# First layer of the compressed keys and values in four 32-column groups, summed by a transposing product

## The chip, the cores and the metric

The kernel runs on one core of one Trainium2 chip. The metric is the device time of one execution in microseconds (us); lower is better. TensorE (PE) multiplies, VectorE (DVE) and ScalarE (ACT) work elementwise, GpSimd (POOL) does small things, and SyncE (SP) issues most of the transfers (DMA).

## The reference, cut to what matters

A decoder trunk of two layers for one sequence of 256 positions and width 1024: attention and a recurrent branch side by side, then a feed-forward part (dense in layer 0, experts in layer 1). One branch of the attention works on compressed keys and values: every window of 32 positions with stride 16 (15 of them per head) is flattened to 2048 numbers and goes through a small two-layer network.

```python
def compress_blocks(kv, pos, w1, w2):
    b_, g_, t_, _ = kv.shape
    ...
    flat = (blocks + pos).reshape(b_, g_, n_cmp, L_CMP * HEAD_DIM)
    return jax.nn.gelu(flat @ w1) @ w2
...
    kc = compress_blocks(grp(k_cmp), cmp_pos[0], cmp_w1[0], cmp_w2[0])
    vc = compress_blocks(grp(v_cmp), cmp_pos[1], cmp_w1[1], cmp_w2[1])
```

`w1` is 2048 x 128, `w2` 128 x 64; keys and values have their own. There are two heads, so keys and values together have 2 x 2 x 15 rows (padded to 2 x 32).

## The kernel before, in words

**Weights.** All weights come from memory as pieces in a fixed list. `emit_load` (line 231) issues a piece's transfer on SP's queue into one of 7 slots of `raw`; `emit_split` and `split_piece` turn a slot into halves of `hl` (5 slots): ACT copies the rounded upper part (line 280), DVE subtracts it and leaves the lower part (line 281). `use` hands a piece to its products and has those of the next piece made. A product with split operands is three PE products (`mm3`, all through `MM`, line 295): upper x upper, upper x lower, lower x upper. The two `w1` pieces of a layer (1 MB each) are not split; they stay in their `raw` slots until their products are done.

**The start.** The 256 positions are two blocks of 128. For each, `Norm.part` squares and sums two halves of a row on ACT and adds up on DVE (`rv`, line 465), `rstd` takes the root on POOL, `scale` (line 481) writes `xn` on DVE in two halves, and `tr` transposes it on PE (line 491) and splits it into `hT` (ACT 495, DVE 496). The first projection, `mixers`' values (`vps`), multiplies `hT` with the two `v` pieces of `w_in`.

**A layer's mixer** (`mixers`, from line 570). In the order of the code: values; recurrent input; `kcvc`; first half of the queries; gates; `flat` (line 731, the windows plus the position term, laid out as 16 chunks of 128 x 32 for keys and for values); `k`; `rg_out(0)`; **the first layer of the compressed keys and values**; `rg_out(1)`; its transpose (line 747) and the second layer; scores and softmax; output projection (`wor`, `woa`). `rg_out` projects a half of the gate branch (48 PE records), applies a Gelu on ACT (`gy`, line 669), multiplies on DVE (670), and makes `sq`, `rech` (ACT) and `recl` (DVE, 677).

**The first layer before.** For keys, then values, 16 products of a chunk (128 x 32, the stationary operand) with 128 rows of `w1` add up in PSUM partitions 0-31 and 32-63. ACT takes the Gelu of the 64 x 128 result into `hid` (744). After `rg_out(1)`, PE transposes `hid` (747) and DVE copies it to `hidt` (749) and spreads the values' part to `vst` (751); both feed the second layer (`w2s`).

**What follows it.** `scores(c)`, four times: PE makes `s`, DVE adds `bias` and takes the minimum in one instruction (792), ACT takes exp (796), DVE scales (803). The softmax over the compressed keys, `pc`, is a chain of DVE steps (854 to 868) with one exp; PE transposes `pc` (882) before the first `attend`.

**What sets the order.** A list scheduler under the code orders each engine's queue; the code's order is its starting point, and `tc.issue_after` holds the instructions in its block behind a named one. So an edit can move instructions that the diff does not touch.

Of the kernel before, what the change touches and what calls it, by code (L numbers as in the profile page):

```python
# [9 lines left out]
F32 = mybir.dt.float32  # L10
# [3 lines left out]
AF = mybir.ActivationFunctionType  # L14
ALU = mybir.AluOpType
# [3 lines left out]
P = 128  # L19
# [35 lines left out]
def f32(ap):  # L55
    return ap.bitcast(F32)
# [3 lines left out]
def decoder_trunk(ctx, tc, x, p, attn_norm, w_in, cmp_pos, cmp_w1, cmp_w2, conv_w, conv_b, lru_wa, lru_ba,  # L60
                  lru_wx, lru_bx, lru_lambda, out_norm_attn, out_norm_rec, w_out, ffn_norm, dense_w_gate,
                  dense_w_up, dense_w_down, router_w, moe_w_gate, moe_w_up, moe_w_down, ple_norm, ple_w_gate,
                  ple_w_proj, final_norm, out, stop=None):
    nc = tc.nc

    const = ctx.enter_context(tc.tile_pool(name="const", bufs=1))
# [6 lines left out]
    def uid(s):  # L73
        cnt[0] += 1
        return f"{s}_{cnt[0]}"

    def pst(s="ps"):
        return psum.tile([P, 512], F32, name=uid(s), tag="ps")
# [116 lines left out]
    keys = {pc[0]: n for n, pc in enumerate(pieces)}  # L195
# [40 lines left out]
    def emit_split(upto):  # L236

        while nsplit[0] <= min(upto, len(pieces) - 1):
            key, srcs, kc, n, split = pieces[nsplit[0]]
            emit_load(nsplit[0])  # L240
            nsplit[0] += 1
            if key[:2] != (DEPTH - 1, "pg"):
                split_piece(key, kc, n, split)
# [43 lines left out]
    def use(*key, ahead=None):  # L287
        emit_split(keys[key] + (depth[0] if ahead is None else ahead))
        split_piece(*[pieces[keys[key]][m] for m in (0, 2, 3, 4)])
        return ready.pop(key)  # L290
# [3 lines left out]
    def MM(*args, **kw):  # L294
        r = nc.tensor.matmul(*args, **kw)  # L295
        if pinned[0]:
            pinned[0] = False
            tc.keep_in_program_order(r)
        return r
# [41 lines left out]
    nc.gpsimd.iota(jp, pattern=[[1, P]], base=0, channel_multiplier=-1, allow_small_or_imprecise_dtypes=True)  # L341
    ident = const.tile([P, P], F32)
    nc.vector.tensor_scalar(ident, jp, 0.0, None, op0=ALU.is_equal)
    tri = const.tile([P, P], F32)
    nc.vector.tensor_scalar(tri, jp, 0.0, None, op0=ALU.is_gt)
    mhalf = const.tile([P, 1], F32)
# [180 lines left out]
    def proj_t(w):  # L527

        ps = pst()
        for ch in range(2):  # L530
            for k in range(KC):
                mm3(ps[:, ch * T:(ch + 1) * T], [v[:, k] for v in w[ch]], (hT[0][:, k, :], hT[1][:, k, :]),
                    k == 0, k == KC - 1)
        return ps
# [40 lines left out]
    def mixers(i, wk, norm, nxt):  # L575
# [7 lines left out]
        flat = [wk.tile([P, 16, 2, 16], F32, name=uid("flat"), tag="flat", bufs=2) for _ in range(2)]  # L583
        qt = wk.tile([P, 4, T], F32, name=uid("qt"), tag="qt", bufs=1)
        kt = wk.tile([P, 2, T], F32, name=uid("kt"), tag="kt", bufs=1)
        bd = wk.tile([P, 2, 4, P], F32, name=uid("bd"), tag="bd", bufs=1)
        hid = wk.tile([64, P], F32, name=uid("hid"), tag="hid", bufs=1)
        wk.tile([P, 1], F32, name=uid("rg"), tag="rg", bufs=NRG)

        vt = wk.tile([P, NB, T], F32, name=uid("vt"), tag="vt", bufs=1)  # L590
# [68 lines left out]
        def rg_scan(hf, a, th, ig, u):  # L659
            nc.scalar.activation(th[sl], th[sl], AF.Sqrt, scale=-0.25)  # L660
            nc.vector.tensor_tensor(ig[sl], ig[sl], th[sl], op=ALU.mult)
            for c in range(2):
                nc.vector.tensor_tensor_scan(u[:, c, :T], a[:, c, :T], ig[:, c, :T], 0.0, op0=ALU.mult, op1=ALU.add)
            return u

        def rg_out(hf, u):
            ps = proj_t(use(i, "yg", hf))
            gy = rgt("gy")
            nc.scalar.activation(gy[:, :, :T], ps.rearrange("p (c t) -> p c t", c=2), AF.Gelu_apprx_tanh)
            nc.vector.tensor_tensor(u[sl], u[sl], gy[sl], op=ALU.mult)  # L670
            sq = rgt("sq", (2, T))
            nc.scalar.activation(sq, u[sl], AF.Square)
            rsq.append(sq)
            for c in range(2):
                cc = 2 * hf + c
                nc.scalar.activation(rec_h[:, cc], u[:, c, :T], AF.Copy, scale=prm(64, cc))
                nc.vector.scalar_tensor_tensor(rec_l[:, cc], u[:, c, :T], prm(64, cc), f32(rec_h[:, cc]),
                                               op0=ALU.mult, op1=ALU.subtract)
# [24 lines left out]
        ps = proj_t(use(i, "kcvc"))  # L703
# [18 lines left out]
        for kv in range(2):  # L722
            ps = pst()
# [10 lines left out]
        ps = proj_t(use(i, "k"))  # L734
        nc.scalar.activation(kt, ps.rearrange("p (v t) -> p v t", v=2), AF.Copy)
        u = [rg_scan(hf, *dec[hf]) for hf in range(2)]
        rg_out(0, u[0])
        hps = pst()
        for kv in range(2):
            w1 = use(i, "w1", kv)  # L740
            for c in range(16):
                MM(hps[kv * 32:kv * 32 + 32, :P], lhsT=flat[kv][:, c].rearrange("p g c -> p (g c)"), rhs=w1[:, c],
                   start=(c == 0), stop=(c == 15))
        nc.scalar.activation(hid, hps[:64, :P], AF.Gelu_apprx_tanh)
        rg_out(1, u[1])
        ps = pst()
        nc.tensor.transpose(ps[:, :64], hid, ident[:64, :64])
        hidt = wk.tile([P, 2, 2, 16], F32, name=uid("hidt"), tag="hidt", bufs=1)
        nc.vector.tensor_copy(hidt, ps[:, :64].rearrange("p (v g c) -> p v g c", v=2, g=2))
        vst = wk.tile([P, 2, 4, 16], F32, name=uid("vst"), tag="vst", bufs=1)  # L750
        nc.vector.tensor_copy(vst, hidt[:, 1, :, None, :].to_broadcast([P, 2, 4, 16]))
        ps = pst()
# [90 lines left out]
        p0 = scores(0)  # L843
# [3 lines left out]
        for c in range(4):  # L847
            for b in range(NB):
                o = (c * 2 + b) * 32
                MM(cps[:, o:o + 32], lhsT=qt[:, c, b * P:(b + 1) * P], rhs=kcb.rearrange("p g k -> p (g k)"),  # L850
                   start=True, stop=True)
# [28 lines left out]
        ps = pst()  # L880
# [20 lines left out]
        norm = Norm(nxt)  # L901
# [24 lines left out]
        for b in range(NB):  # L926
            for hf in range(2):
                if b == 0:
                    ps = ps0[hf]
                    wo_mm(ps, att, b, w[hf], (3,))  # L930
                else:
                    ps = pst()
# [15 lines left out]
            if router and b:  # L948
# [5 lines left out]
                r = norm.rstd(b)  # L954
                for hf in range(2):
                    v = norm.x[b][:, hf * 512:hf * 512 + 512]
# [614 lines left out]
    def dump():  # L1571
        for b in range(NB):
            nc.sync.dma_start(out[0, b * P:(b + 1) * P, :], xt[:, b])

    norm = Norm(None, gain0)
    for b in range(NB):
        for hf in range(2):
            norm.half(b, hf)
        norm.scale(b)
        if b == 0:  # L1580
            norm.tr(b)
    for i in range(DEPTH):
        with tc.tile_pool(name=f"att{i}", bufs=1, reuse_waits="tile") as wk:
            norm = mixers(i, wk, norm, ffn_norm[i])
        if stop == f"mix{i}":
            return dump()
        with tc.tile_pool(name=f"ffn{i}", bufs=1, reuse_waits="tile") as wk:
            if i == 0:
                ppj, prev = dense(i, wk, norm)
            else:  # L1590
                more = [(hpool, "hT0", 1), (hpool, "hT1", 1)] + [(ring, "raw", NRAW)] * (NRAW - NEARLY)
                more += [(bpool, "bias", 1)] + [(wk, "raw2", NRAW2)] * NRAW2 + [(ring, "hl", NSPL)] * NSPL
                more += [(ring, "raw", NRAW)] * NEARLY
                slots[:] = itertools.cycle(more), wk
                moe(i, wk, norm)
            if i == 0 and stop != "ffn0":
                norm = Norm(attn_norm[i + 1])
                ple(i, wk, ppj, prev, norm)
        if stop == f"ffn{i}":
            return dump()  # L1600
        if stop == f"ple{i}":
            return dump()
# [30 lines left out]
```

## Time and profile before

| | us |
|---|---|
| median of 3 runs | 1388.51 (1386.14 to 1388.85) |
| the profiled execution | 1390.27 |
| its span, first to last instruction | 1388.6 |
| around the span | 1.67 |
| mean granted TensorE clock | 0.984 of full speed |

The profile is of one execution, 1.76 us above the median of the runs. PE is busy for 93% of the span, DVE 45%, ACT 37%, POOL 3%. In the page's 40 slices of 34.7 us, the DMA engines stand at 9 tenths or more in the first two slices, at 1 to 6 tenths in the third to the fourteenth, and at 9 or more again from the fifteenth to the last but one. A busy PE is not PE at its peak: the ends of matmuls are modelled. A product in full 32-bit floats leaves two records per instruction in the trace, so the 32 products of a first layer are 64 records.

### The profile page before, as it was taken

To read this page: it belongs to the slowest core of one execution; us is meant where nothing else is said; L and a number is where in the kernel's file an instruction comes from. 1 tells how busy PE (TensorE), PEld (TensorE's weight loads), DVE (VectorE), ACT (ScalarE), POOL (GpSimd) and SP (SyncE) were. 2 spreads that over 40 slices of the span, in tenths; PEclk is the share of its full clock that TensorE was granted. 3 is DMA by queue.
4 is the path that set the end of the run, shared out by engine and by line. 5 is a ranking of instruction groups with operands and counts; after the bars stand their busy time and mean duration, and the time that the engine had idled before them with its cause. 6 is when DMAs were issued, how large, how long until landed. Compare 5 with 4: busy or idle time off the path is not lost. (4 is left out here: it accounts for less than half of the span.)

```text
span 1388.6 us, 18284 instructions
## 1 busy us (share of the span) xinstructions
PE 1296.0 (93%) x7056; PEld 825.1 (59%) x7056; DVE 618.4 (45%) x1036; ACT 514.5 (37%) x808; POOL 35.8 (3%) x72
## 2 busy tenths in 40 slices
PE   7999999999999989999999999999879788788996
PEld 6977899998897743568753468854323222233432
DVE  7866655546777530278841178842010011013203
ACT  5665544445566520357730157740000010002103
POOL 2000000000100000000000000000000000000000
PEclk9999999999999999999999999999989999999998
DMA  9941555554646399999999999999999999999992
GB/s 281 265 132 62 205 184 190 192 192 125 203 141 165 124 394 404 396 393 394 402 408 410 396 394 395 395 410 409 402 408 409 402 409 381 394 403 403 393 390 99
DMA packets 180615, 435.83 MB, mean 314 GB/s; under 512 B 8841, under 2 KB 59177, under 8 KB 180522
## 3 DMA queue, kind: packets, MB, share of 16 engines
q1 hardware_dynamic: 178984, 430.92, 83.4%
q0 software_dynamic: 992, 3.15, 0.7%
q8 instruction: 58, 0.95, 0.3%
q10 hardware_dynamic: 546, 0.53, 0.1%
q14 instruction: 35, 0.29, 0.1%
HBM read 433.51 MB, written 1.05 MB: 313 GB/s over the span
## 5 line engine op out<-in xcount | busy, mean ns | idle before, releaser
L281 DVE TENSOR_TENSOR hl<-raw,hl 128x1024 fp32r<-128x1024 f32 (+1 forms) x294 | 343.9, 1206 | 147.6 <-ACT hl L280 141.8
L295 PE MATMUL gu<-raw,x 128*64 128x512 f32 (+1 forms) x1536 | 315.4, 554 | 36.9 <-DMA raw<-in_moe_w_up_dram 15.0
L280 ACT ACTIVATE hl<-raw 128x1024 fp32r<-128x1024 f32 (+1 forms) x294 | 294.2, 1043 | 113.5 <-PE ps L295 67.2
L295 PEld LDWEIGHTS gu<-raw,x 128*64 128x64 f32 x1536 | 107.2, 139 | 225.6 <-issue 158.5
L295 PE MATMUL ps<-hT,hl 128*128 128x256 f32 x1824 | 221.5, 281 | 1.2 <-ACT hT L495 0.8
L295 PEld LDWEIGHTS ps<-hT,hl 128*128 128x128 f32 x1824 | 217.9, 188 | 4.0 <-ACT hT L495 1.0
L1286 DVE TENSOR_TENSOR sl<-sl,gu 128x512 f32<-128x512 f32 (+1 forms) x24 | 14.9, 621 | 414.9 <-PE gu L295 381.9
L295 PE MATMUL y<-raw,at 128*64 128x512 f32 x672 | 157.3, 599 | 8.0 <-DMA raw<-in_moe_w_down_dram 7.9
L295 PE MATMUL gu<-hl,xh 128*128 128x512 f32 x448 | 144.4, 398 | 1.9 <-ACT hl L280 1.7
L295 PEld LDWEIGHTS y<-raw,at 128*64 128x64 f32 x672 | 45.2, 136 | 100.3 <-issue 78.5
L295 PEld LDWEIGHTS gu<-hl,xh 128*128 128x128 f32 x448 | 83.7, 188 | 34.1 <-DVE hl L281 9.5
L1285 ACT ACTIVATE sl<-gu 128x512 f32<-128x512 f32 (+1 forms) x24 | 13.1, 544 | 240.0 <-PE gu L295 240.0
L295 PE MATMUL gu<-hl,xl 128*128 128x512 f32 x224 | 88.0, 393 | 0.0
L295 PE MATMUL y<-hl,ah 128*128 128x512 f32 x224 | 73.2, 399 | 0.0
L295 PE MATMUL ps<-hl,hT 128*128 128x512 f32 (+1 forms) x288 | 64.9, 377 | 0.5 <-ACT hT L524 0.5
L1295 ACT ACTIVATE at<-ps 128x512 f32<-128x512 f32 (+1 forms) x24 | 13.1, 544 | 132.5 <-PE ps L1293 132.5
L295 PEld LDWEIGHTS ps<-hl,hT 128*128 128x128 f32 x288 | 49.7, 197 | 19.8 <-issue 10.0
L295 PE MATMUL acc<-hl,ah 128*128 128x512 f32 x176 | 55.5, 397 | 0.0
L295 PEld LDWEIGHTS y<-hl,ah 128*128 128x128 f32 x224 | 41.6, 188 | 10.8 <-issue 1.6
L295 PEld LDWEIGHTS gu<-hl,xl 128*128 128x128 f32 x224 | 42.1, 188 | 8.1
L295 PE MATMUL y<-hl,al 128*128 128x512 f32 x112 | 43.9, 392 | 0.0
L295 PEld LDWEIGHTS acc<-hl,ah 128*128 128x128 f32 x176 | 32.2, 188 | 6.9
(312 smaller groups left out, 1091.4 us busy)
## 6 DMA issues: line engine op xcount, KB each, us to landing
raw<-in_moe_w_gate_dram SPq DMA_DIRECT2D x112, 1024.0 KB
raw<-in_moe_w_up_dram SPq DMA_DIRECT2D x112, 1024.0 KB
raw<-in_moe_w_down_dram SPq DMA_DIRECT2D x112, 1024.0 KB
raw<-in_dense_w_gate_dram SPq DMA_DIRECT2D x11, 1024.0 KB
raw<-in_dense_w_up_dram SPq DMA_DIRECT2D x11, 1024.0 KB
raw<-in_dense_w_down_dram SPq DMA_DIRECT2D x11, 1024.0 KB
raw<-in_w_in_dram SPq DMA_DIRECT2D x10, 1024.0 KB
raw<-in_ple_w_gate_dram SPq DMA_DIRECT2D x8, 1024.0 KB
```

The costliest lines, as they stand in the source:

```text
L280: done[0] = nc.scalar.activation(ho, src, AF.Copy)
L281: done[1] = nc.vector.tensor_tensor(lw, src, f32(ho), op=ALU.subtract)
L295: r = nc.tensor.matmul(*args, **kw)
L1285: nc.scalar.activation(sl[:, :nh], pg[:, :nh], AF.Silu)
L1286: nc.vector.tensor_tensor(sl[:, :nh], sl[:, :nh], pu[:, :nh], op=ALU.mult)
L1295: nc.scalar.activation(at[:, :nh], ps[:, :nh], AF.Copy)
```

## The change

In the first layer of the compressed keys and values, keys and values are taken in turn, and of each the even and the odd chunks add up apart: output partitions `kv * 64 + m * 32`, four groups of 32 columns of PE. `hid` is then 128 x 128 and a plain copy. Instead of the transpose, one product with a constant `pair` (128 x 64, two ones in each column) adds the even and odd sums and transposes. The Gelu now comes after it, on ACT, and writes `hidt`; DVE's copy is gone. At the start, the split of the first `v` piece is put behind the first block's scaling.

```diff
--- before.py
+++ after.py
@@ -341,6 +341,9 @@
     nc.gpsimd.iota(jp, pattern=[[1, P]], base=0, channel_multiplier=-1, allow_small_or_imprecise_dtypes=True)
     ident = const.tile([P, P], F32)
     nc.vector.tensor_scalar(ident, jp, 0.0, None, op0=ALU.is_equal)
+    pair = const.tile([P, 2, 32], F32)
+    idv = ident.rearrange("p (v m r) -> p v m r", v=2, m=2)
+    nc.vector.tensor_tensor(pair, idv[:, :, 0], idv[:, :, 1], op=ALU.add)
     tri = const.tile([P, P], F32)
     nc.vector.tensor_scalar(tri, jp, 0.0, None, op0=ALU.is_gt)
     mhalf = const.tile([P, 1], F32)
@@ -584,7 +587,7 @@
         qt = wk.tile([P, 4, T], F32, name=uid("qt"), tag="qt", bufs=1)
         kt = wk.tile([P, 2, T], F32, name=uid("kt"), tag="kt", bufs=1)
         bd = wk.tile([P, 2, 4, P], F32, name=uid("bd"), tag="bd", bufs=1)
-        hid = wk.tile([64, P], F32, name=uid("hid"), tag="hid", bufs=1)
+        hid = wk.tile([P, P], F32, name=uid("hid"), tag="hid", bufs=1)
         wk.tile([P, 1], F32, name=uid("rg"), tag="rg", bufs=NRG)
 
         vt = wk.tile([P, NB, T], F32, name=uid("vt"), tag="vt", bufs=1)
@@ -735,18 +738,22 @@
         nc.scalar.activation(kt, ps.rearrange("p (v t) -> p v t", v=2), AF.Copy)
         u = [rg_scan(hf, *dec[hf]) for hf in range(2)]
         rg_out(0, u[0])
+
         hps = pst()
-        for kv in range(2):
-            w1 = use(i, "w1", kv)
-            for c in range(16):
-                MM(hps[kv * 32:kv * 32 + 32, :P], lhsT=flat[kv][:, c].rearrange("p g c -> p (g c)"), rhs=w1[:, c],
-                   start=(c == 0), stop=(c == 15))
-        nc.scalar.activation(hid, hps[:64, :P], AF.Gelu_apprx_tanh)
+        w1 = [use(i, "w1", kv) for kv in range(2)]
+        for c in range(0, 16, 2):
+            for kv in range(2):
+                for m in range(2):
+                    p0 = kv * 64 + m * 32
+                    MM(hps[p0:p0 + 32, :P], lhsT=flat[kv][:, c + m].rearrange("p g c -> p (g c)"),
+                       rhs=w1[kv][:, c + m], start=(c == 0), stop=(c == 14), skip_group_check=True)
+        nc.scalar.activation(hid, hps[:, :P], AF.Copy)
         rg_out(1, u[1])
+
         ps = pst()
-        nc.tensor.transpose(ps[:, :64], hid, ident[:64, :64])
+        MM(ps[:, :64], lhsT=hid, rhs=pair.rearrange("p v r -> p (v r)"), start=True, stop=True)
         hidt = wk.tile([P, 2, 2, 16], F32, name=uid("hidt"), tag="hidt", bufs=1)
-        nc.vector.tensor_copy(hidt, ps[:, :64].rearrange("p (v g c) -> p v g c", v=2, g=2))
+        nc.scalar.activation(hidt, ps[:, :64].rearrange("p (v g c) -> p v g c", v=2, g=2), AF.Gelu_apprx_tanh)
         vst = wk.tile([P, 2, 4, 16], F32, name=uid("vst"), tag="vst", bufs=1)
         nc.vector.tensor_copy(vst, hidt[:, 1, :, None, :].to_broadcast([P, 2, 4, 16]))
         ps = pst()
@@ -1579,6 +1586,9 @@
         norm.scale(b)
         if b == 0:
             norm.tr(b)
+
+            with tc.issue_after(norm.last.ins):
+                emit_split(keys[(0, "v", 0)])
     for i in range(DEPTH):
         with tc.tile_pool(name=f"att{i}", bufs=1, reuse_waits="tile") as wk:
             norm = mixers(i, wk, norm, ffn_norm[i])
```

Three places in the instruction order. PE, layer 0, the first layer of the compressed keys and values (`flat` is the stationary operand, `raw` a slot with `w1`, `hT` and `hl` the projections around it); before:

```order
L295 MATMUL ps_736<-hT_158,hl_673 128x256
L295 MATMUL ps_794<-raw_734,flat_189 32x128 x16
L295 MATMUL ps_794<-raw_795,flat_190 32x128 x16
L295 MATMUL ps_847<-hT_158,hl_815 128x256
L295 MATMUL ps_847<-hT_159,hl_815 128x256
L295 MATMUL ps_847<-hT_158,hl_815 128x256 x2
```

and with the change:

```order
L295 MATMUL ps_738<-hT_160,hl_675 128x256
L295 MATMUL ps_796<-raw_736,flat_197 32x128 x2
L295 MATMUL ps_796<-raw_797,flat_198 32x128 x2
L295 MATMUL ps_796<-raw_736,flat_197 32x128 x2
L295 MATMUL ps_796<-raw_797,flat_198 32x128 x2
L295 MATMUL ps_796<-raw_736,flat_197 32x128 x2
L295 MATMUL ps_796<-raw_797,flat_198 32x128 x2
L295 MATMUL ps_796<-raw_736,flat_197 32x128 x2
L295 MATMUL ps_796<-raw_797,flat_198 32x128 x2
L295 MATMUL ps_796<-raw_736,flat_197 32x128 x2
L295 MATMUL ps_796<-raw_797,flat_198 32x128 x2
L295 MATMUL ps_796<-raw_736,flat_197 32x128 x2
L295 MATMUL ps_796<-raw_797,flat_198 32x128 x2
L295 MATMUL ps_796<-raw_736,flat_197 32x128 x2
L295 MATMUL ps_796<-raw_797,flat_198 32x128 x2
L295 MATMUL ps_796<-raw_736,flat_197 32x128 x2
L295 MATMUL ps_796<-raw_797,flat_198 32x128 x2
L295 MATMUL ps_849<-hT_160,hl_801 128x256
```

The same 32 instructions stand between the same neighbours; two of keys and two of values now alternate.

DVE at the start (`rv` is the sum of squares, `xn` the scaled block, `hl` the lower parts of the `v` pieces, `hT` the split of the transposed block); before:

```order
L281 TENSOR_TENSOR hl_198<-raw_75,hl_198 128x560
L281 TENSOR_TENSOR hl_201<-raw_75,hl_201 128x560
L465 TENSOR_SCALAR rv_176<-ss_174 128x1
L343 TENSOR_SCALAR ident<-jp 128x128
L345 TENSOR_SCALAR tri<-jp 128x128
L481 SCALAR_TENSOR_TENSOR xn_144<-xt,rr_154,gain_85 128x512
L481 SCALAR_TENSOR_TENSOR xn_144<-xt,rr_154,gain_87 128x512
L465 TENSOR_SCALAR rv_180<-ss_178,rv_176 128x1
L281 TENSOR_TENSOR hl_204<-raw_80,hl_204 128x560
L481 SCALAR_TENSOR_TENSOR xn_145<-xt,rr_182,gain_85 128x512
```

and with the change:

```order
L468 TENSOR_SCALAR rv_184<-ss_182 128x1
L343 TENSOR_SCALAR ident<-jp 128x128
L348 TENSOR_SCALAR tri<-jp 128x128
L346 TENSOR_TENSOR pair<-ident 128x64
L484 SCALAR_TENSOR_TENSOR xn_146<-xt,rr_156,gain_85 128x512
L484 SCALAR_TENSOR_TENSOR xn_146<-xt,rr_156,gain_87 128x512
L281 TENSOR_TENSOR hl_176<-raw_75,hl_176 128x560
L281 TENSOR_TENSOR hl_179<-raw_75,hl_179 128x560
L499 TENSOR_TENSOR hT_161<-ps_162,hT_160 128x4x128
L499 TENSOR_TENSOR hT_161<-ps_169,hT_160 128x4x128
L468 TENSOR_SCALAR rv_188<-ss_186,rv_184 128x1
L281 TENSOR_TENSOR hl_206<-raw_80,hl_206 128x560
L484 SCALAR_TENSOR_TENSOR xn_147<-xt,rr_190,gain_85 128x512
```

The two lower parts of the first piece moved from ahead of the first block's scaling to behind it, `rv` of the second block from ahead of the first split of `hT` to behind it. ACT's order at the start is the same in both: the squares of the first block, the two upper parts of the first piece, the squares of the second block.

DVE in layer 0 behind the second half of the gate branch (`hidt`, `vst`, `kcb`, `vcr`, `vcb` belong to the compressed keys and values; `recl` and `u` to the recurrent branch; `e`, `nm` to the scores; `hl_1213` is the lower part of the first half of `wor`'s second piece); before:

```order
L749 COPY hidt_907<-ps_905 128x64
L751 COPY vst_909<-hidt_907 128x128
L670 TENSOR_TENSOR u_650<-u_650,gy_896 128x2x256
L792 ISA e_122_929,nm_940<-s_125_932,bias 128x256
L792 ISA nm_940 128x1
L760 COPY kcb_915<-ps_911 64x16 x2
L762 COPY vcr_919<-ps_911 128x64
L792 ISA e_122_929,nm_940<-s_125_932,bias 128x256
L792 ISA nm_940 128x1
L677 SCALAR_TENSOR_TENSOR recl_291<-u_650,par,rech_290 128x256 x2
L764 TENSOR_TENSOR vcb_921<-vcr_919,vmask 128x512
```

and with the change:

```order
L673 TENSOR_TENSOR u_652<-u_652,gy_898 128x2x256
L758 COPY vst_911<-hidt_909 128x128
L281 TENSOR_TENSOR hl_1213<-raw_1211,hl_1213 128x1024
L680 SCALAR_TENSOR_TENSOR recl_293<-u_652,par,rech_292 128x256 x2
L767 COPY kcb_917<-ps_913 64x16 x2
L769 COPY vcr_921<-ps_913 128x64
L799 ISA e_122_931,nm_942<-s_125_934,bias 128x256
L799 ISA nm_942 128x1
L771 TENSOR_TENSOR vcb_923<-vcr_921,vmask 128x512
```

The copy of `hidt` is gone, and a lower part of the `wor` weights and both `recl` now stand ahead of the first score reduction. That lower part stood before inside the chain of `pc`, between the sum `cs` and its reciprocal (the row at 443.26 in the section below is its place in layer 1); in its place there, one more score reduction of `scores(1)` now stands ahead of the end of `pc`. On ACT, `hidt` stands behind `gy` of the second half and ahead of the upper parts of that weight.

## Rows read from the trace of the kernel before

**Rows 1.** The page: busy time by engine, share of the span, instructions

```profile
PE 1296.0 (93%) x7056; PEld 825.1 (59%) x7056; DVE 618.4 (45%) x1036; ACT 514.5 (37%) x808; POOL 35.8 (3%) x72
```

**Rows 2.** Windows: span, PE, PEld, DVE, ACT, POOL busy, PEclk, DMA share, GB/s

```profile
61.40:68.20 6.80, 6.80 (x66) 6.57 (x65) 4.77 (x6) 2.97 (x5) 0.97 (x1) 1.00 0.83 190
...
140.00:360.00 220.00, 216.77 (x1462) 197.93 (x1460) 121.87 (x137) 106.68 (x138) 4.00 (x6) 1.00 0.55 181
...
490.00:1388.60 898.60, 825.12 (x3847) 411.99 (x3845) 302.15 (x392) 250.10 (x338) 3.67 (x9) 0.98 1.00 388
```

**Rows 3.** Timeline of PE from 55 to 80 us: start, busy time, instruction

```profile
61.44 6.77 PE L295 MATMUL ps<-raw,flat 128*32 128x128 f32 x64
68.13 5.92 PE L295 MATMUL ps<-hT,hl 128*128 128x256 f32 x48
```

**Rows 4.** Instructions on tile flat and on hid: ns min/median/max, first and last start

```profile
L295 PEld LDWEIGHTS ps<-raw,flat x128: 106/110/110, 61.4 to 420.4; 128*32 128x32 f32 x128
...
L744 ACT ACTIVATE hid<-ps x2: 271/271/271, 68.2 to 420.9; 64x128 f32<-64x128 f32 x2
```

**Rows 5.** Instructions on tile pt, and timeline at 100.62: a group in two column groups

```profile
L295 PE MATMUL ps<-pt,vt x192: 272/273/323, 97.7 to 478.0; 128*64 128x128 f32 x192
...
100.62 1.09 PE L295 MATMUL ps<-pt,vt 128*64 128x128 f32 x16
```

**Rows 6.** Timeline of layer 1 from 414 to 428: flat group, second half's products, hidt

```profile
414.05 6.77 PE L295 MATMUL ps<-raw,flat 128*32 128x128 f32 x64
...
420.75 5.92 PE L295 MATMUL ps<-hT,hl 128*128 128x256 f32 x48
...
426.60 0.27 PE L747 MATMUL ps<-ident,hid 64*128 64x64 f32 x1
426.76 0.60 ACT L669 ACTIVATE gy<-ps 128x512 f32<-128x512 f32 x1 [1.82 <-PE ps L295]
426.90 0.22 DVE L749 COPY hidt<-ps 128x64 f32<-128x64 f32 x1 [0.70 <-PE ps L747]
```

**Rows 7.** Timelines of layers 1 and 0: DVE's work before the transposes of pc

```profile
428.57 0.42 DVE L792 CUSTOM_DVE_ANT_0 e<-s,bias 128x256 f32<-128x256 f32 x1 [0.49 <-PE s L295]
...
429.88 1.60 DVE L677 SCALAR_TENSOR_TENSOR recl<-u,par,rech 128x256 fp32r<-128x256 f32 x2
...
443.26 1.22 DVE L281 TENSOR_TENSOR hl<-raw,hl 128x1024 fp32r<-128x1024 f32 x1
...
446.01 0.41 PE L882 MATMUL ps<-ident,pc 128*128 128x128 f32 x2 [2.01 <-DVE sums L801]
...
96.07 0.41 PE L882 MATMUL ps<-ident,pc 128*128 128x128 f32 x2 [1.55 <-DVE sums L801]
```

**Rows 8.** Timeline of the start, 7 to 18 us

```profile
7.71 1.23 ACT L280 ACTIVATE hl<-raw 128x560 fp32r<-128x560 f32 x2 [2.70 <-DMA raw<-in_w_in_dram]
8.41 1.39 DVE L281 TENSOR_TENSOR hl<-raw,hl 128x560 fp32r<-128x560 f32 x2 [3.15 <-ACT hl L280]
...
9.72 0.15 DVE L465 TENSOR_SCALAR rv<-ss 128x1 f32<-128x1 f32 x1
...
10.05 1.40 DVE L481 SCALAR_TENSOR_TENSOR xn<-xt,rr,gain 128x512 f32<-128x512 f32 x2
...
17.93 3.35 PE L295 MATMUL ps<-hl,hT 128*128 128x280 f32 x24
```

**Rows 9.** Timelines of SP's queue and ACT in layer 1: the loads of w_out

```profile
416.89 5.21 SPq L231 DMA_DIRECT2D raw<-in_w_out_dram  x5
...
427.87 1.06 ACT L280 ACTIVATE hl<-raw 128x1024 fp32r<-128x1024 f32 x1 [0.51 <-DMA raw<-in_w_out_dram]
```

**Rows 10.** Windows, as rows 2: the clock's fall in layer 0, both layers' tails

```profile
74.00:96.10 22.10, 20.24 (x105) 14.65 (x105) 16.70 (x70) 14.51 (x42) 2.18 (x3) 0.85 0.35 111
...
86.70:93.50 6.80, 6.80 (x17) 4.28 (x17) 5.20 (x24) 3.84 (x17) 0.00 (x0) 0.50 0.00 0
...
420.80:446.00 25.20, 22.88 (x152) 18.46 (x152) 19.13 (x72) 16.80 (x45) 2.25 (x3) 1.00 0.63 139
```

## The prediction

> **What bounds the kernel now.** I read the page first, for engines and stages, then busy time in windows that cut the program into stages, then the timelines of the stretches that the change touches, and the waits in them. PE is the busiest engine [rows 1], but what ends last differs by stage. From 490 us to the end the DMA share is 1.00 [rows 2]: the experts' weights stream for 898.6 us, and nothing in the change touches that stream. It starts when the earlier work lets go of its buffers, so time saved ahead of it moves it forward, about one for one. In the dense stage (140 to 360 us) PE is busy for 216.77 of 220.00 us at a DMA share of 0.55 [rows 2]: PE sets the pace, and a microsecond saved in layer 0 passes through. The attention stretches where the change lies are PE's too, with one wait in each that DVE ends, that of the transposes of `pc`: 1.55 us in layer 0, 2.01 us in layer 1 [rows 7].
>
> In the first layer of the compressed keys and values PE is busy throughout, 6.80 of 6.80 us [rows 2]. The group runs from 61.44 us to the next projection's start at 68.13 [rows 3], 6.69 us for 64 records, 0.105 us each; in layer 1 from 414.05 to 420.75, 6.70 us [rows 6]. Each product fills only 32 of PE's 128 columns.
>
> **Term A, the four groups.** The trace has no group in four column groups. Its nearest is `pt,vt`, in two groups of 64 columns with the same 128 moving columns: 16 records in 1.09 us, the last of 0.273 us [rows 5]. With two records side by side that is 8 slots, (1.09 - 0.273) / 7 = 0.117 us a slot, about what one record of `flat` costs alone. So a second group came for next to nothing. With four side by side, 64 records are 16 slots: 16 x 0.117 = 1.87 us, a gain of 4.82 us a layer. Bounds: two side by side only, 32 x 0.117 = 3.74 us, a gain of 2.95; one after another, none; and a loss if the weight loads stop overlapping (third rival). I take 4.82, since `pt,vt` is the nearest row and differs only in the number of groups.
>
> **Term B, sum and transpose.** The transpose of `hid`, 0.27 us at 426.60 [rows 6], becomes a product of an instruction of two records, some 0.43 us. It lies beside `gy` on ACT, which runs from 426.76 to 427.36 [rows 6], and costs nothing of its own; without that cover 0.16. The copy into `hid` (0.27 us, as the Gelu took [rows 4]) lies under the 5.92 us of the next projection.
>
> **Term C, the Gelu.** Before, DVE had `hidt` at 426.90 + 0.22 = 427.12 us, beside `gy`. Now ACT makes it behind `gy`: 427.36 plus 0.27 (the former Gelu on fewer partitions but more columns [rows 4]) = 427.63. The second layer's products wait for it on PE with the scores queued behind: +0.51 us a layer. Bounds: +0.2, if the products of the scores go ahead, and +1.0, if ACT's own queue is late.
>
> **Term D, DVE's queue.** The scheduler moved one lower part of the `wor` weights (1.22 us [rows 7]) out of the chain of `pc` to a place ahead of the first score reduction, and put one more reduction of 0.42 us [rows 7] into that chain. PE waits 1.55 and 2.01 us there, so it is worth -1.22 + 0.41 = -0.81 us a layer. Bounds: -1.2 if the reduction is hidden; and +1.6, if the lower part (1.21) and `recl` (1.60 [rows 7]), both now ahead of the first reduction, delay the exps and with them everything up to `pc`: 2.81 less the 1.22 that went. I take -0.81: DVE is free for a part of each wait in that stretch (19.13 busy of 25.20 us [rows 10]).
>
> **Term E, the start.** The lower parts (2 pieces, 1.39 us) leave DVE's queue ahead of the first scaling, which began at 10.05 us [rows 8]. But `rv` of the second block still stands ahead of it; it ran at 9.72 and waits for ACT, whose squares stand behind the upper parts that wait for DMA at 7.71 [rows 8]. So the scaling starts at about 10.1 as before. The 1.39 us then come between it and the split of `hT`, in time that PE's and ACT's work on the transposes partly covers, and the second block's scaling slips. The last values' products begin at 17.93 [rows 8] and can absorb part. I take +0.3; bounds -0.3 (the scaling starts earlier by the constants' work) and +1.2 (nearly all of 1.39 shows). `pair`, one DVE instruction of 64 columns, is inside that.
>
> **Term F, the loads of w_out in layer 1.** SP issues five of them at 416.89 us, 5.21 us in all, and ACT, when it took the first one's data at 427.87, had waited 0.51 us for DMA [rows 9]. With the group 4.83 us shorter, ACT asks at about 427.36 + 0.27 - 4.8 = 422.8. The `raw` slots that hold `w1` come free earlier too, by as much, but this piece did not wait for all of them. The loss lies between 0 and 5.0; from 416.89 plus the 5.21 us of issue the data could be there at 422.1 to 424.5. I take +1.5. Layer 0's trace shows no such wait.
>
> **The sum.** 2 x (-4.82 + 0.51 - 0.81) = -10.24; + 0.3 + 1.5 gives -8.44. On the profiled execution 1390.27 - 8.44 = 1381.83; that execution lies 1.76 above the median of the runs, so the median should be **1380.1 us**.
>
> One thing that I can't size is the clock. In layer 0 the granted clock stood at 0.50 (1.2 GHz of 2.4) from 86.7 to 93.5 us, after PE had stood idle and run short groups; in layer 1's like stretch it stayed at 1.00 [rows 10]. From the flat group's end to the transposes of `pc` took 96.07 - 68.13 = 27.94 us in layer 0 and 446.01 - 420.75 = 25.26 in layer 1 [rows 3, 6, 7]: a fall costs some 2.7 us. Less work ahead of that stretch may take the fall away, or bring one to layer 1. I take none of it and put 2.7 on both sides.
>
> **Rivals.** *First: two side by side only*, because PE takes up no more records a time than `pt,vt` shows, (1.09 - 0.273) / 15 = 0.054 us a record. For it: no row shows a higher rate. Against: in `pt,vt` the columns were full with two. It costs 16 slots more a layer, 2 x 1.87 = 3.74: 1383.8 us. The Trainium skill ("TensorE: Matmul & The Clock Gate", "Wait — 56ns, not 53.3ns?") names about 62 ns a matmul as a bound where the sequencer decodes in software; by an estimate from that the group takes 64 x 0.062 = 3.97 us. The trace's 0.054 is already below it.
>
> *Second: the loads of w_out bound layer 1* (term F at its end): 5.0 us there instead of 1.5, so +3.5, 1383.6 us. For it: ACT already waited 0.51. Against: the loads are issued 11 us ahead of their use.
>
> *Third, on the other side: weight loads no longer overlap.* Each record loads its 32 columns in 0.110 us [rows 4]. Before, the loads were busy for 6.57 of 6.80 us beside the products [rows 2]. If alternating the groups makes a load wait for the products in flight, a record costs 0.110 + 0.106 and the group 64 x 0.216 = 13.8 us, 7.1 more a layer and not 4.82 less: 2 x 11.95 = 23.9 above the forecast, less term F's 1.5, which then vanishes: 1402.5 us. With F gone the other terms sum to -0.30, so the change is slower than before from 6.84 us a group, 0.107 us a record; slower by over 0.2% from 0.129. Against it: `pt,vt` alternates two groups and pays nothing. The Trainium skill (same page, "The mechanism") says that a load overlaps products in flight only where its row group differs; all four groups here use all rows, so by that rule this rival holds. The trace disagrees: before, loads and products of the same rows overlapped.
>
> *Fourth: it doesn't do what it says*, the four groups run one after another at 0.105 us a record as now: the other terms alone, 1388.5 - 0.3 = 1388.2 us.
>
> **How the numbers follow.** Forecast 0.55, first rival 0.17, second 0.16, third 0.06, fourth 0.06. Low end: the forecast with D at its good end (-0.8 in both layers), F at 0 (-1.5) and the clock's fall gone (-2.7): 1375.1. High end: the first rival with one more fall (+2.7): 1386.5. Beyond it lie the third and fourth rivals, 0.12, and the tails. 0.2% is 2.8 us, about what a measurement of this kernel can tell from no change: faster means below 1385.7. The forecast's cases all do, three in four of the first two rivals': 0.55 + 0.75 x 0.33 = 0.80. Within 0.2% are the rest of these, 0.08, and the fourth: 0.14. Slower: the third, 0.06.
>
> **What would show it.** Right: the group of 64 records at 61.4 and near 409 us takes 1.8 to 2.2 us; `hidt` on ACT ends some 0.27 behind `gy`; PE's wait before the transposes of `pc` falls below 1.55 and 2.01; ACT waits 1 to 2 us for `w_out` in layer 1; the stream of the experts' weights starts some 8 us earlier and lasts as long. Wrong: a group of 3.5 us or more, a start over 1 us longer, a DMA wait of 4 us in layer 1, or a stream that starts earlier and ends where it did.

## The result, and the profile after

The changed kernel takes 1378.07 us (median of 11 runs, 1375.58 to 1385.40) against 1388.51 before; the ratio is 0.9933, with a 95% interval of 0.9919 to 0.9947. That is 9.3 us, and the interval 7.4 to 11.2; the two medians lie 10.4 apart. Timed again (run 8 below) it was 0.9933 once more. The forecast was 1380.1 us, in a range of 1375.1 to 1386.5.

The profiled execution took 1378.07 us, its span 1376.4 (1388.6 before). First the group that was changed, in the timeline of PE: start, busy time, instruction.

```profile
62.93 1.96 PE L295 MATMUL ps<-raw,flat 128*32 128x128 f32 x64
64.81 5.92 PE L295 MATMUL ps<-hT,hl 128*128 128x256 f32 x48
70.57 0.33 PE L295 MATMUL ps<-pair,hid 128*128 128x64 f32 x2
71.59 0.29 PE L295 MATMUL ps<-hidt,w2s 128*64 128x16 f32 x4 [0.69 <-ACT hidt L756]
```

The 64 records run from 62.93 to the next projection at 64.81, 1.88 us where [rows 3] had 6.69. Layer 1 shows the same group, and what comes behind it:

```profile
407.48 1.69 PEld L295 LDWEIGHTS ps<-raw,flat 128*32 128x32 f32 x64
407.48 1.95 PE L295 MATMUL ps<-raw,flat 128*32 128x128 f32 x64
...
409.36 5.92 PE L295 MATMUL ps<-hT,hl 128*128 128x256 f32 x48
...
415.38 0.60 ACT L672 ACTIVATE gy<-ps 128x512 f32<-128x512 f32 x1 [1.12 <-PE ps L295]
...
415.88 0.22 ACT L756 ACTIVATE hidt<-ps 128x64 f32<-128x64 f32 x1
...
416.66 1.06 ACT L280 ACTIVATE hl<-raw 128x1024 fp32r<-128x1024 f32 x1 [0.57 <-DMA raw<-in_w_out_dram]
...
434.30 0.41 PE L889 MATMUL ps<-ident,pc 128*128 128x128 f32 x2 [1.34 <-DVE sums L805]
```

The weight loads fell with the products, from 6.57 us busy [rows 2] to 1.69. `hidt` now ends behind `gy`, and PE waits 0.69 us for it. The wait before the transposes of `pc` fell from 2.01 [rows 7] to 1.34, and ACT's wait for `w_out` is 0.57, as it was [rows 9]. In windows of the changed kernel (the columns of [rows 2]):

```profile
136.00:354.00 218.00, 215.78 (x1457) 196.88 (x1455) 119.91 (x135) 104.44 (x135) 3.23 (x5) 1.00 0.55 181
477.80:1376.40 898.60, 824.63 (x3850) 413.06 (x3849) 302.40 (x393) 250.17 (x338) 3.67 (x9) 0.98 1.00 389
86.70:93.50 6.80, 5.46 (x35) 3.56 (x33) 6.80 (x27) 4.09 (x15) 0.00 (x0) 1.00 0.21 65
```

The dense stage and the stream of the experts' weights are as before, only earlier. The third window is new: the clock that had stood at 0.50 near 90 us in layer 0 [rows 10] stays at 1.00, and this trace has no fall between 14.8 and 363 us.

Where the 12.2 us between the two profiled spans are, from the starts of the same PE instructions in both traces:

| stretch | before | after | difference |
|---|---|---|---|
| start to the flat group, layer 0 | 61.44 | 62.93 | +1.49 |
| flat group, layer 0 | 6.69 | 1.88 | -4.81 |
| its end to the products with `w2s` | 6.44 | 6.78 | +0.34 |
| from there to the transposes of `pc` | 21.50 | 18.16 | -3.34 |
| from there to the flat group of layer 1 | 317.98 | 317.73 | -0.25 |
| flat group, layer 1 | 6.70 | 1.88 | -4.82 |
| its end to the products with `w2s` | 6.43 | 6.79 | +0.36 |
| from there to the transposes of `pc` | 18.83 | 18.15 | -0.68 |
| from there to the end | 942.59 | 942.10 | -0.49 |

The -3.34 in layer 0 holds the clock: layer 1 gained 0.68 in the same stretch, and the other 2.66 is the fall that this execution does not have. Run 3, which has DVE's order of before and no fall in layer 0, takes 18.83 us there and not 21.50.

### The profile page after: what moved, and what is told of

It reads as the page before. It is cut to its first block, busy times and chain, and to the rows that moved or that the text cites. A ratio compares the mean times of both kernels' runs of the same rounds, so it can differ in the third digit from the quotient of the medians.

```text
span 1376.4 us, 18290 instructions
## 1 busy us (share of the span) xinstructions
PE 1280.9 (93%) x7058; PEld 813.2 (59%) x7058; DVE 618.2 (45%) x1035; ACT 514.0 (37%) x810; POOL 37.5 (3%) x72
## 5 line engine op out<-in xcount | busy, mean ns | idle before, releaser
L1293 DVE TENSOR_TENSOR sl<-sl,gu 128x512 f32<-128x512 f32 (+1 forms) x24 | 14.9, 620 | 412.8 <-PE gu L295 379.7
```

Source lines behind the costliest of these rows:

```text
L1293: nc.vector.tensor_tensor(sl[:, :nh], sl[:, :nh], pu[:, :nh], op=ALU.mult)
```

## The experiments

**Runs 1 and 2: the start edit, taken out and alone.** Run 1 is the changed kernel without these lines, run 2 the kernel before with them.

```diff
             norm.tr(b)
-
-            with tc.issue_after(norm.last.ins):
-                emit_split(keys[(0, "v", 0)])
```

> The changed kernel without its edit at the start (the split of the first v piece is placed by the scheduler again; all else as changed). In the changed kernel's profile the flat group of layer 0 starts at 62.93 us and not 61.44: 0.25 us of that is there by the end of the first projection (21.37 against 21.12), the other 1.24 is a wait of ACT for a piece of w_in at 49.15 (1.49 us, 0.25 before). Theory S: both come from the start edit, since the first raw slot comes free some 2.7 us later and the saturated stream of transfers is behind from there on. Then the flat group here starts at 61.2 to 61.7, ACT waits under 0.5 us for that piece, and the time is 1.0 to 1.5 us below the changed kernel. Rival T: only the 0.25 comes from the edit and the late piece is a matter of the single execution. Then the flat group starts anywhere from 61.2 to 62.9 and the time is 0.0 to 0.4 us below.

> The kernel before with the start edit alone. Theory S: the flat group of layer 0 starts at 62.6 to 63.2 us (61.44 before) and the time is 1.0 to 1.5 us above the kernel before. Rival T: 61.5 to 61.9, and 0.2 to 0.4 us above. Third: the edit gains by itself (the first scaling earlier); then the first transposes start before 10.65 us and the time is below the kernel before.

Run 1: ratio to before 0.9952 (0.9934 to 0.9971), so the edit's removal did not make the changed kernel (0.9933) faster. Run 2: 1.0016 (1.0001 to 1.0031), slower than before by 2.2 us with an interval that almost reaches none. The times alone leave the edit's worth open. The traces say more, once all executions are set side by side. Three marks: SP's release from its wait for a `w_in` piece (start of the transfer of `out_norm_attn`), PE's end of the values (start of the transpose of `prow`), and the flat group of layer 0. The last column is the moment at which the trace's record of the granted clock begins, at 1.00; the products of the values (128x280) start 0.233 us apart before it and 0.13 us apart behind it.

| kernels | SP goes on | values end | flat group | clock at 1.00 from |
|---|---|---|---|---|
| without the edit: before, runs 1, 3, 6 | 14.34, 13.61, 13.77, 14.10 | 21.12, 20.64, 20.31, 20.95 | 61.44, 61.61, 61.12, 61.86 | 15.03, 15.08, 13.23, 15.01 |
| with it: after, runs 2, 4, 5, 8 | 15.00, 15.08, 15.57, 14.58, 15.04 | 21.37, 21.79, 21.58, 21.90, 21.79 | 62.93, 62.46, 62.85, 62.52, 61.78 | 14.82, 15.81, 14.98, 16.20, 16.22 |

The means of the first three marks differ by 1.10, 0.93 and 1.00 us. So kernels with the edit come to the flat group about 1 us later, though run 8's 61.78 lies among those without it. How much of this is there when the values end stays open. Both of my theories had 0.25 from one pair of traces, and the means say 0.93, but the executions with the edit also happened to have the full clock later. Where it came at nearly the same time (before, runs 1 and 6 against after and run 4), the values end 0.57 us later and the flat group starts 1.25 later. Of theory S's marks, the flat group's came in run 1 (61.61) and was just missed in run 2 (62.46); ACT's wait for the late `w_in` piece was 0.90 us in run 1 and not under 0.5. The third theory's mark came in run 2, with the first transposes at 10.46 us, but the shorter time did not.

**Run 3: two groups, nothing else.** The kernel before with keys and values alternating; DVE's and ACT's orders are those of before.

```diff
-        for kv in range(2):
-            w1 = use(i, "w1", kv)
-            for c in range(16):
-                MM(hps[kv * 32:kv * 32 + 32, :P], lhsT=flat[kv][:, c].rearrange("p g c -> p (g c)"), rhs=w1[:, c],
-                   start=(c == 0), stop=(c == 15))
+        w1 = [use(i, "w1", kv) for kv in range(2)]
+        for c in range(16):
+            for kv in range(2):
+                MM(hps[kv * 32:kv * 32 + 32, :P], lhsT=flat[kv][:, c].rearrange("p g c -> p (g c)"), rhs=w1[kv][:, c],
+                   start=(c == 0), stop=(c == 15), skip_group_check=True)
```

> The kernel before with keys and values alternating in the first layer of the compressed keys and values: two column groups of 32, no even and odd sums, the transpose and the Gelu where they were. Theory P (records in different column groups run side by side, one slot of 0.117 us for as many groups as alternate): 32 slots, 3.5 to 3.75 us a group, 2.95 to 3.2 less than 6.69 in both layers; neither the late hidt (0.5 us a layer) nor the moved lower part is in it, and the time is 5.9 to 6.4 us below the kernel before. Rival Q (what matters is a rate of records, 0.03 us each as measured with four): 1.9 to 2.3 us a group already, 9 us below. Rival R (32 columns alone don't run side by side; the four-group gain comes from the halves): 6.7 us a group, no gain.

Timeline of PE, both layers' groups and the wait before the transposes of `pc`:

```profile
61.12 3.69 PE L295 MATMUL ps<-raw,flat 128*32 128x128 f32 x64
64.74 1.52 PE L295 MATMUL ps<-hT,hl 128*128 128x256 f32 x11
...
406.28 3.69 PE L295 MATMUL ps<-raw,flat 128*32 128x128 f32 x64
409.90 2.27 PE L295 MATMUL ps<-hT,hl 128*128 128x256 f32 x17
...
435.17 0.41 PE L882 MATMUL ps<-ident,pc 128*128 128x128 f32 x2 [2.02 <-DVE sums L801]
```

3.62 us in both layers, and a ratio of 0.9950 (0.9932 to 0.9968), 6.9 us: theory P. Two groups nearly halve the 6.69 us and four nearly quarter it, so up to four PE's limit is the slot, not a rate of records. What sets the slot stays open: records of one column group start 0.109 us apart, and a weight load lasts 0.110 us. The wait of 2.02 us for DVE is untouched here, and with the change it is 1.34: that part comes with DVE's new order, not with the groups.

**Run 4: four groups, one after another.** The changed kernel with its loops turned.

```diff
-        for c in range(0, 16, 2):
-            for kv in range(2):
-                for m in range(2):
+        for kv in range(2):
+            for m in range(2):
+                for c in range(0, 16, 2):
```

> The changed kernel with the loops turned: the four groups are the same and add up in the same partitions, but each group's 8 products are issued together, one group after the other; every other instruction is in the same place. Theory P (side by side needs alternation in the issue order): the group takes 6.6 to 6.8 us as before the change, hence 4.8 more a layer than in the changed kernel, and the time is 9 to 10 us above the changed kernel, about that of the kernel before. Rival U (PE looks far enough ahead to bring groups together): 1.9 to 3 us, the time of the changed kernel.

```profile
62.85 5.95 PE L295 MATMUL ps<-raw,flat 128*32 128x128 f32 x64
68.74 1.45 PE L295 MATMUL ps<-hT,hl 128*128 128x256 f32 x10
...
410.53 5.95 PE L295 MATMUL ps<-raw,flat 128*32 128x128 f32 x64
416.42 1.80 PE L295 MATMUL ps<-hT,hl 128*128 128x256 f32 x13
```

5.89 us, 4.0 more than in the changed kernel, and a ratio of 0.9991 (0.9973 to 1.0008): nearly the whole gain is gone although the groups, their sums and every other instruction are the same. So the alternation is what counts. Theory P's 6.6 was too high by 0.7, and U has a small part in it: where one group ends and the next begins, some eight records start 6, 103, 30 and 79 ns apart in place of 109, so a few records of two groups do run side by side. The kernel before shows the same at its one boundary, between keys and values.

**Runs 5 and 6: the Gelu ahead of `gy`.** The summing product and `hidt` go between the two halves of the next projection's products; run 6 also leaves out the start edit.

```diff
-        rg_out(1, u[1])
-
-        ps = pst()
-        MM(ps[:, :64], lhsT=hid, rhs=pair.rearrange("p v r -> p (v r)"), start=True, stop=True)
-        hidt = wk.tile([P, 2, 2, 16], F32, name=uid("hidt"), tag="hidt", bufs=1)
-        nc.scalar.activation(hidt, ps[:, :64].rearrange("p (v g c) -> p v g c", v=2, g=2), AF.Gelu_apprx_tanh)
+        hidt = wk.tile([P, 2, 2, 16], F32, name=uid("hidt"), tag="hidt", bufs=1)
+
+        def hid_tr():
+            ph = pst()
+            MM(ph[:, :64], lhsT=hid, rhs=pair.rearrange("p v r -> p (v r)"), start=True, stop=True)
+            nc.scalar.activation(hidt, ph[:, :64].rearrange("p (v g c) -> p v g c", v=2, g=2), AF.Gelu_apprx_tanh)
+
+        rg_out(1, u[1], hid_tr)
...
         for ch in range(2):
+            if ch and mid is not None:
+                mid()
```

> The changed kernel with the summing, transposing product and the Gelu of hidt put between the two halves of the next projection's products (after 24 of 48 records), so that ACT takes the Gelu ahead of gy and not behind it. Theory C (the late hidt holds PE for 0.69 us before w2s and costs 0.45 us a layer): PE's wait before w2s falls to 0.2 or less, the distance from the flat group's end to w2s from 6.78 to about 6.25 us, and the time by 0.9 to 1.1. Rival: the scores' products and DVE's queue set the pace there; the wait moves to the products of w2s with vst or to the transposes of pc, and the time stays within 0.3.

> The kernel of the run before, and the edit at the start left out. If both costs are real and add (1.3 at the start, 0.9 to 1.1 for hidt), it is 2 to 2.5 us below the changed kernel, timed again beside it. If the start edit costs nothing in the time, 0.9 to 1.1; if neither, the same.

Run 5: 1375.36 us, ratio to before 0.9903 (0.9887 to 0.9919), 3.9 us below the changed kernel timed beside it (1379.25), where 0.9 to 1.1 was expected; the interval overlaps that kernel's (0.9909 to 0.9957) a little. Run 6: 1376.57, 0.9906 (0.9890 to 0.9921). The start edit makes no difference between them that the times can show, so run 6's 2.7 us falls near the expected 2 to 2.5 for another reason. PE in layer 1 of run 5:

```profile
409.91 0.33 PE L295 MATMUL ps<-pair,hid 128*128 128x64 f32 x2
410.05 3.07 PE L295 MATMUL ps<-hT,hl 128*128 128x256 f32 x24
413.05 0.29 PE L295 MATMUL ps<-hidt,w2s 128*64 128x16 f32 x4
413.51 0.43 PE L295 MATMUL ps<-w2s,vst 128*128 128x64 f32 x2 [0.16 <-DVE vst L763]
413.87 1.56 PE L295 MATMUL s<-kt,qt 64*128 64x512 f32 x8
...
429.58 0.41 PE L894 MATMUL ps<-ident,pc 128*128 128x128 f32 x2 [0.52 <-DVE pc L880]
```

The same scores in the changed kernel, and then in the kernel before:

```profile
416.37 1.12 PE L295 MATMUL s<-kt,qt 64*128 64x512 f32 x2
417.43 0.43 PE L295 MATMUL ps<-w2s,vst 128*128 128x64 f32 x2
417.79 1.55 PE L295 MATMUL s<-kt,qt 64*128 64x512 f32 x6
...
427.41 1.12 PE L295 MATMUL s<-kt,qt 64*128 64x512 f32 x2
428.46 0.43 PE L295 MATMUL ps<-w2s,vst 128*128 128x64 f32 x2
428.82 1.55 PE L295 MATMUL s<-kt,qt 64*128 64x512 f32 x6
```

The place of `hidt` is worth more than PE's 0.69 us of waiting. With it early, the scheduler puts the second layer's products ahead of all the scores, and the eight records of the scores run in one piece: 1.56 us in place of 1.12 + 1.55. In the other two kernels a product over all 128 rows stands between the first score product, which uses 64 rows, and its partner; in the changed kernel these two start 1.42 us apart, in run 5 0.007 us. From the products with `w2s` to the first product behind the scores that is 2.32 us and not 3.12. PE's wait for DVE before `pc` falls too, from 1.34 to 0.52. From the flat group's end to the transposes of `pc` layer 1 takes 22.60 us (6.07 + 16.53) and not 24.94 (6.79 + 18.15), and layer 0 22.26 and not 24.94. Theory C had the direction and 0.45 of the 2.3 us a layer. Only the 0.36 us of waiting in it is a loss of the change made good: the kernel before has its scores in two pieces too, and takes 25.26 us there in layer 1.

**Run 7: POOL's small transfers put back.** The changed kernel; three of the four transfers of `bd` wait for POOL's root of the second block, as they stood before, and the next two transfers of POOL's stay behind them.

```diff
-                nc.gpsimd.dma_start(bd[s * 64:(s + 1) * 64, v, :, s * 64:(s + 1) * 64],
-                                    wv[i].rearrange("(c s) k n -> s k c n", s=2)[s])
+                with behind(i, norm.pw if v + s else None):
+                    held[0] = nc.gpsimd.dma_start(bd[s * 64:(s + 1) * 64, v, :, s * 64:(s + 1) * 64],
+                                                  wv[i].rearrange("(c s) k n -> s k c n", s=2)[s])
```

> The changed kernel, start edit included, with three of POOL's four transfers of bd held behind POOL's root for the second block, as they stood before the change (64 KB each, issued at 12.7 to 14.6 us before, at 7.6 to 10.2 since); all other engines keep their order. Theory M (the edit made the second block's sum late, the scheduler drew the small transfers ahead of the root, and they hold up the w_in loads): SP gets on from its wait for a w_in piece at 6.6 to 6.9 us after ACT's first split (kernels without the edit: 6.63, 6.91, 6.74; with it: 7.54, 7.63, 7.86), the last w_in piece of that stretch is taken at 47.3 to 48.0 and not 48.7 to 49.2, and the flat group starts at 61.5 to 62.2, with most of the 1.3 us back. Rival N (DVE's two moved subtractions or the late transposes delay the stream): 7.5 or more, and the flat group at 62.9 or later.

PE and SP at the start of run 7; the first row has the first 19 products of the values, which in the changed kernel took 3.95 us, and the third the end of the values:

```profile
12.16 5.01 PE L300 MATMUL ps<-hl,hT 128*128 128x280 f32 x19
13.84 0.61 SPq L388 DMA_DIRECT2D prow<-in_out_norm_attn_dram  x2
22.14 0.27 PE L371 MATMUL ps<-ident,prow 128*128 128x128 f32 x1
...
62.13 1.95 PE L300 MATMUL ps<-raw,flat 128*32 128x128 f32 x64
```

SP goes on at 13.84 us, 6.68 behind ACT's first split at 7.16, where the five executions with the edit have 7.48 to 7.96: theory M for that wait. The last `w_in` piece is taken at 48.31, between M's range and the other, and the flat group starts at 62.13, inside M's range and 0.4 before the mean with the edit. But the values end at 22.14, later than in any other execution. This one had the full clock last of all, from 16.93 us, and its first 19 products took 1.06 us more than the changed kernel's. So the small transfers hold up SP by about 1.0 us; whether they cost PE anything, this run does not tell. What makes PE later with the edit, the second block's scaling behind the two subtractions or something else in that stretch, no run took apart.

Its time was 1382.48 us (0.9945, 0.9924 to 0.9967), from four runs that do not tell it from the changed kernel's 0.9933. The profiled execution lost time in layer 1. Windows there (the columns of [rows 2]):

```profile
418.40:421.80 3.40, 3.40 (x15) 3.11 (x15) 3.34 (x16) 1.69 (x7) 0.23 (x1) 0.50 1.06 211
...
432.00:435.40 3.40, 3.40 (x9) 2.25 (x8) 2.54 (x18) 3.16 (x15) 0.00 (x0) 0.50 0.00 0
```

The clock stood at 0.50 in two stretches of layer 1, and from `w2s` to the transposes of `pc` took 24.48 us there; the changed kernel and runs 1, 4 and 8 have 18.15 or 18.16 there.

**Run 8: the changed kernel again**, unchanged.

> The changed kernel once more, beside the three above on the same chip. The flat group takes 1.88 us in both layers again; whether the clock falls near 85 us in layer 0 is open: with it the way from w2s to the transposes of pc takes about 21 us there, without it 18.15, and the time differs by 2.7 to 3.

1.88 us in both layers; from `w2s` to `pc` 18.16 us in both, no fall. Ratio 0.9933 (0.9909 to 0.9957), the seven runs from 1374.74 to 1387.52 us.

## Why the prediction was right, point by point

**What bounds it** held. The dense stage is as PE-bound as before, the experts' stream as long, and what was saved ahead of it moved it forward: of -11.71 us at layer 1's transposes of `pc`, -12.20 arrive at the end. (Some 8 us earlier was forecast for the stream.)

**Term A, the four groups**, was right to the hundredth: 1.88 us measured, 1.87 forecast, from the slot of `pt,vt`. The slot is right, the hundredth is luck: inside the group a slot is 0.109 us and not 0.117, and the first one (0.134) and the last, up to the next projection's first product (0.223), are longer. Runs 3 and 4 show the reason and not only the size: a slot of some 0.11 us holds one record of each group that alternates (3.62 us with two groups, 1.88 with four, 5.89 with four that do not alternate). In the changed kernel's records four starts lie within 20 ns, and the next four 109 ns behind them.

**Term B** lay under other work as said. **Term C** was +0.51 a layer, measured +0.34 and +0.36: `hidt` took 0.22 us and not 0.27, and started before `gy` had ended, so that it was done 0.12 us behind it. But I priced the wait alone: run 5 shows that the place of `hidt` decides the order of the scores too, and that 2.3 us a layer hang on it.

**Term D** was -0.81, measured -0.68 in layer 1, as a wait of 1.34 in place of 2.01; run 3, with DVE's order of before, kept its 2.02, and its 18.83 us in layer 0 against 18.16 give the same there. The bad bound of +1.6 did not come up.

**Term E, the start**, was +0.3 and is about +1.0 by nine traces. In the profiled execution it was 1.49, beyond the bound of +1.2 and a sign of being wrong by the prediction's own list (a start over 1 us longer). The mis-sized step is the one that puts the 1.39 us of lower parts between the first scaling and the split of `hT` and lets the second block's scaling slip. The lower parts did not hold up the split: it began at 12.47 us and not 13.44. The second scaling slipped by 2.4 us; before and with the change:

```profile
12.78 0.75 DVE L481 SCALAR_TENSOR_TENSOR xn<-xt,rr,gain 128x512 f32<-128x512 f32 x1 [0.46 <-POOL rr L473]
13.44 1.28 DVE L496 TENSOR_TENSOR hT<-ps,hT 128x512 fp32r<-128x512 f32 x2
...
12.47 1.50 DVE L499 TENSOR_TENSOR hT<-ps,hT 128x512 fp32r<-128x512 f32 x2
15.20 1.41 DVE L484 SCALAR_TENSOR_TENSOR xn<-xt,rr,gain 128x512 f32<-128x512 f32 x2 [0.46 <-POOL rr L476]
```

How much of the 1.0 us this slip makes is not shown. A second thing was overlooked: POOL's transfers of `bd` moved ahead of its root, and SP waits about 1.0 us longer; run 7 leaves open whether PE pays for that. A third was the full clock's later start in some of these executions.

**Term F, the loads of w_out**, was +1.5 and is about nothing: ACT's wait for the data was 0.51 us and is 0.57 (0.46 to 0.94 in the profiles of runs 1, 5, 6, 7 and 8, none in those of runs 2, 3 and 4). The step that failed took the loads' issue as fixed at 416.89 us. SP waits for slots that the splits set free: DVE's instruction of line 281 is what it waits for, 16.4 of 17.5 us in the trace of before and all 18.0 in that of the changed kernel, and the splits came earlier with all the rest. Nor are the loads five, as the prediction had it, but six. Before, and with the change:

```profile
413.46 8.64 SPq L231 DMA_DIRECT2D raw<-in_w_out_dram  x6
...
406.88 7.15 SPq L231 DMA_DIRECT2D raw<-in_w_out_dram  x6
```

The first is issued 6.6 us earlier, and the last is out at 414.03 and was at 422.10, 8.1 us earlier. ACT takes the data 11.2 us earlier, at 416.66 and not 427.87, with about the same wait: the loads kept up.

**The sum.** -8.44 was forecast for the profiled execution and -12.2 came. The clock's fall, which I had kept out as 2.7 on either side, is 2.66 of the difference; F's 1.5 and C's 0.3 help, E's 1.2 in that execution and D's 0.3 go against it, and 0.7 lies in the dense stage and the experts' stream, where the executions of one kernel differ by more (from layer 1's transposes of `pc` to the end the changed kernel took 942.1 us in one and 944.2 in the other). Over all runs 9.3 us came, 0.9 more than forecast. With the terms as measured and no fall of the clock the sum is 2 x (-4.82 + 0.35 - 0.68) + 1.0 = -9.3. So the forecast is close in part because errors cancel: F was 1.5 us and C 0.3 us too high, E 0.7 us and D 0.3 us too low.

**The rivals.** The first (pairs only) falls with 1.88 us in place of 3.74. The estimate of 3.97 us by the Trainium skill ("TensorE: Matmul & The Clock Gate", "Wait — 56ns, not 53.3ns?") falls with it, but it took the 62 ns that the page gives for a matmul decoded in software for each record. A product leaves two records, so by that figure the group would be estimated at 32 x 0.062 = 1.98 us, and the 1.88 measured is only just below that; the 0.054 us a record of `pt,vt`, 0.109 a product, spoke neither for nor against it. The second (loads) falls with the 0.57 us. The third (weight loads in the way) falls with the 1.69 us of loads in a group of 1.88: each set of four loads starts within 0.02 us of the start of four products over the same rows and lasts as long as their slot. So the sentence of the Trainium skill (same page, "The mechanism") that loads overlap products in flight only where the row group differs does not hold here. The fourth is nearly what run 4 shows: groups one after another take 5.89 us and not 6.69, and its 0.9991 is the 1388.2 us worked out for that rival within the measurement.

## What to carry to other kernels

Here products with 32 stationary columns were worth splitting into four column groups, and the groups had to alternate in the issue order: the same groups one after another gave 0.8 us of 4.8. The nearest multi-group row in one's own trace, read as a slot and not as a rate of records, gave the price. A small step that moves to another engine (here a Gelu of 0.22 us) is to be looked at for what the scheduler then puts in front of what, and not only for its wait.

## What was not expected of the hardware

The granted clock fell to 0.50 (1.2 GHz) in layer 0's stretch before the transposes of `pc` in the profiled executions of before and of runs 1 and 2, twice in layer 1's in run 7, and in neither layer's in those of the changed kernel and of runs 3 to 6 and 8. A fall costs 2.7 to 3.0 us in layer 0 (21.50 us against 18.83 with the order of before, 21.19 against 18.15 with the change), and the two in run 7 6.3. What PE did ahead of it does not tell which execution has one. Just ahead of the fall in the kernel before PE was busy for 3.40 of 3.40 us, with 25 records (83.3 to 86.7 us), so the idle time that the prediction names is not seen there. Ahead of the first fall in run 7 it was busy for 2.71 of 3.40 us (412.8 to 416.2). Run 8 has the same order of PE's instructions as run 7, and no fall. The moment at which its record begins, at 1.00, moves too, from 13.23 to 16.93 us in the ten profiled executions. Neither was under control in any run, so comparisons of single executions of this kernel carry some 3 us of the falls.
